# A hybrid decoder layer on one core: norms' root in the output stage, a longer run of products at the switch to the MLP, and more buffers for reloaded activations

## The chip, the cores and the metric

The kernel runs on one core of a Trainium2 chip. The metric is device time in microseconds (us), the median of several executions. A profile of one execution goes with it; its times count from the start of its span.

The engines are TensorE (PE for matmuls, PEld for weight loads), VectorE (DVE), ScalarE (ACT), GpSimd (POOL) and SyncE (SP). SP does no arithmetic here: it is a queue that issues DMA transfers in order. Each engine works through its own list in order, so an instruction that waits holds up everything behind it on that engine.

## The reference, cut to what matters

One decoder layer runs over 1024 prompt tokens and 32 sample tokens (T = 1056 columns, model width 1024, MLP width 4096, all float32). The change lies in the second half of the layer:

```python
x = x + merged @ w_out
h2 = rmsnorm(x, g_ffn)
x = x + jnp.square(jax.nn.relu(h2 @ w_up)) @ w_down
...
y = rmsnorm(x, g_final)
```

## The kernel before, in words

Activations lie transposed, channels on partitions and tokens along the free dimension. The 1056 tokens fall into four column blocks of 264 (CQ), and a "quarter" c (0 or 1) is the pair of blocks (t, c) for t = 0, 1. A float32 product is made of three matmuls: each operand is split into a rounded part (a copy on ACT) and a rest (a subtraction on DVE), and high x high, high x low and low x high are summed in one PSUM bank.

**Output stage** (out_quarter, lines 1167 to 1190). For each quarter, eight row blocks m of x + merged @ w_out are computed. Each adds its squares to `acc` (ACT line 1163, GpSimd line 1164). After each pair of row blocks j, `factors` makes the seven combined right operands of a 2x2x2 fast product (Winograd's form of Strassen) from the pair. The splits in it are line 1133 (ACT) and line 1134 (DVE).

**Up stage** (16 groups, class Up). Group u makes 256 rows of the hidden layer by seven products i = 0 to 6 per quarter. A "unit" is one group for one quarter; a product in it is 12 matmuls of 264 columns (line 1231). Products 0, 3, 5 and 6 sum in one bank `x` and products 2 and 4 in a bank `z`; after each, ACT or DVE copies the bank out, and the next product into that bank waits for the copy. The tokens' norm factors enter in `relu2` (line 1254) as `rb2`. They come from `column_norms`: matmuls with a vector of ones (line 1198), a root and a Newton step (lines 157 to 162), matmuls that spread the result over the partitions (line 1204), a copy into `rb2` (line 1206). The tile of `rb2` takes the memory of `acc`. Hidden values go to DRAM (`ffd`).

**Down stage** (16 windows, class Down). A window accumulates 2 to 4 hidden groups into the 256 output rows `mp`. Its right operands come back from `ffd`: `right` (line 1387) loads one into a buffer "gt" (line 1392, from SP; two buffers), ACT rounds it (line 1394) and DVE makes the rest (line 1395). There are 98 such loads; the last one or two windows' worth are held in 28 of 29 large buffers (slabA with 20, slabB with 9). The residual x returns from DRAM into `accs`, and DVE adds the products to it (lines 1306 to 1309). The weights are factored on ACT and DVE five steps ahead (lines 1341 to 1351). The last 512 hidden rows take an ordinary product at the end, with the final norm.

PSUM has two pools, `mmbank` with three banks and `bank` (tiles "ax") with five. A scheduler in the framework decides each engine's order from priorities in program order and free buffers; it also picks which freed buffer a tile gets.

Of the kernel before, what the change touches and what calls it, by code (L numbers as in the profile page):

```python
# [8 lines left out]
F32 = mybir.dt.float32  # L9
F32R = mybir.dt.float32r  # L10
# [6 lines left out]
P = 128  # L17
# [6 lines left out]
T = SEQ + NS  # L24
# [21 lines left out]
def hybrid_kernel(tc, xt, cache_k, cache_v, h0, norms, w_in, sinks, w_attn_o, lam_re, lam_im, log_dt,  # L46
                  b_ri, b_ir, c_ri, d_cols, w_glu, w_out, w_up, w_down, w_last,
                  y_cols, y_rows, k_prompt, v_prompt, ssm_prompt, k_sample, v_sample, ssm_sample, dbg=None):
    nc = tc.nc
    uid = [0]  # L50

    def new(pool, shape, dt, tag, bufs=None):
        uid[0] += 1
        return pool.tile(list(shape), dt, tag=tag, name=f"{tag}_{uid[0]}", bufs=bufs)
# [3 lines left out]
    wts = es.enter_context(tc.tile_pool(name="wts", bufs=2))  # L58
# [3 lines left out]
    slabA = es.enter_context(tc.tile_pool(name="slabA", bufs=20))  # L62

    def bank(pool=None):
        return new(psax, [P, 512], F32, "ax")

    def mmbank():
        return new(psmm, [P, 512], F32, "mm")
# [11 lines left out]
    ps = bank()  # L80
# [74 lines left out]
    def rsqrt_newton(out, ms, tmp1, tmp2):  # L155

        nc.scalar.activation(tmp1, ms, AF.Sqrt)
        nc.vector.reciprocal(tmp1, tmp1)  # L158
        nc.vector.tensor_tensor(tmp2, tmp1, tmp1, op=ALU.mult)
        nc.vector.tensor_tensor(tmp2, tmp2, ms, op=ALU.mult)  # L160
        nc.vector.tensor_scalar(tmp2, tmp2, -0.5, 1.5, op0=ALU.mult, op1=ALU.add)
        nc.vector.tensor_tensor(out, tmp1, tmp2, op=ALU.mult)
# [360 lines left out]
    with tc.tile_pool(name="ptmp", bufs=1) as pt:  # L523
        with tc.tile_pool(name="start", bufs=1) as st:
            prm = []
            acc = start(st, lambda: prm.extend(s5_small_loads(pt)))
# [3 lines left out]
            ft = s5_params(pt, *prm)  # L530
# [543 lines left out]
    slabB = es.enter_context(tc.tile_pool(name="slabB", bufs=9, side="right", reuse_waits="tile"))  # L1074
# [3 lines left out]
    for k in range(KT):  # L1078
        a = q2[k // 2][:, k % 2]
        h = new(slabB, [P, T], F32R, "slab")  # L1080
        l = new(slabA, [P, T], F32R, "slab")
# [5 lines left out]
    HT, CQ = T // 2, T // 4  # L1087
# [40 lines left out]
    def factors(j, c, x, pools):  # L1128

        V = nc.vector  # L1130

        def split(t, src):
            nc.scalar.copy(t[:, :, 0], src)
            V.tensor_tensor(t[:, :, 1], src, t[:, :, 0].bitcast(F32), op=ALU.subtract)

        b, t14, t3 = (new(p, [P, 2, 2, CQ], F32R, "slab") for p in pools[:3])
        if c == 0:
            odd[j] = new(pools[3], [P, 2, 2, CQ], F32R, "slab")
        split(b, x[:, :, 0])
        V.tensor_tensor(x[:, 0, 0], x[:, 0, 1], x[:, 0, 0], op=ALU.subtract)  # L1140
        t2 = new(wts, [P, 2 * CQ], F32, "gt")[:, :CQ]
        V.tensor_tensor(t2, x[:, 1, 1], x[:, 0, 0], op=ALU.subtract)
        V.tensor_tensor(x[:, 1, 0], x[:, 1, 0], t2, op=ALU.subtract)
        V.tensor_tensor(x[:, 0, 1], x[:, 1, 1], x[:, 0, 1], op=ALU.subtract)
        split(t14, x[:, :, 0])
        split(odd[j][:, c:c + 1], t2.rearrange("p (o f) -> p o f", o=1))
        split(t3, x[:, :, 1])
        h2c[c][j] = [b[:, 0], b[:, 1], t14[:, 0], odd[j][:, c], t3[:, 1], t3[:, 0], t14[:, 1]]
# [23 lines left out]
    def out_quarter(c, last_weights):  # L1172
        w = wblock(w_out, 0)
        for j in range(KT // 2):
            xr = new(gen, [P, 2, 2, CQ], F32, "slab")
            x = new(gen, [P, 2, 2, CQ], F32, "slab")
            for i in range(2):
                m = 2 * j + i
                nc.sync.dma_start(xr[:, i], quarter(xt[m], c))
                last = c == 1 and m == KT - 1  # L1180
                wm = w
                if m + 1 < KT:
                    w = wblock(w_out, m + 1)
                else:
                    last_weights()
                out_tile(wm, m, c, xr[:, i], last or c == m == 0, bank if last else mmbank)
                nc.scalar.activation(x[:, i], xr[:, i], AF.Copy, scale=gcol[:, 1, m:m + 1])
                nc.sync.dma_start(quarter(x2d[j][:, i], c), xr[:, i])
            factors(j, c, x, FPOOLS[c][j])

    def column_norms(c):

        n = CQ // 3
        ms, r, t1, t2 = (small4(6, tag=t, bufs=2) for t in ("nms", "nr", "nt1", "nt2"))
        ps = bank()
        for i in range(6):
            t0 = (i // 3) * HT + c * CQ + (i % 3) * n
            nc.tensor.matmul(ps[:n, i:i + 1], acc[:, t0:t0 + n], ones[:, 0:1], start=True, stop=True)
        nc.vector.tensor_scalar(ms[:n], ps[:n, :6], 1.0 / D, EPS, op0=ALU.mult, op1=ALU.add)
        rsqrt_newton(r[:n], ms[:n], t1[:n], t2[:n])  # L1200
        for t in range(2):
            ps = bank()
            for i in range(3):
                nc.tensor.matmul(ps[:, i * n:i * n + n], r[:n, 3 * t + i:3 * t + i + 1].to_broadcast([n, P]),
                                 ident[:n, :n], start=True, stop=True)
            nc.scalar.copy(rb2[c][:, t], ps[:, :CQ])

# [10 lines left out]
    class Unit:  # L1218
# [15 lines left out]
        def step(self, i):  # L1234
            if i == 0:
                self.x = ps = bank()
            elif i == 1:
                ps = mmbank()
            elif i == 2:
                self.z = ps = mmbank()  # L1240
            else:
                ps = self.z if i == 4 else self.x
            self.prod(ps, i, i < 3)
            self.take(i, ps[:, :CQ])
# [133 lines left out]


    fct = {}  # L1380
    PLACES = [slabA] * 6 + [slabB] * 3 + [slabA] * 2 + [slabB] * 2 + [slabA] * 6 + [slabB] * 2 + [slabA] * 6 + [slabB]
    rights = []
    for n, (_, _, u1) in enumerate(WINDOWS):
        u0 = max([0] + [w[2] for w in WINDOWS[:n]])
# [2 lines left out]
    def right(n):  # L1387

        for _ in range(n):
            u, i = rights.pop(0)  # L1390
            ft = new(wts, [P, 2, CQ], F32, "gt")
            nc.sync.dma_start(ft, ffd[u][:, SLOT[i]])
            f = fct[u, i] = new(PLACES[(7 * u + i) % 28], [P, 2, 2, CQ], F32R, "slab")
            nc.scalar.copy(f[:, 0], ft)  # L1394
            V.tensor_tensor(f[:, 1], ft, f[:, 0].bitcast(F32), op=ALU.subtract)  # L1395
# [4 lines left out]
    rbt = new(const, [P, 2, 2, CQ], F32, "rb")  # L1400
    for c in range(2):
        rb2[c] = rbt[:, c]
    accs = {2: new(accp, [P, 2, T], F32, "acc")}
    nc.sync.dma_start(accs[2], x2d[2])

# [1 line left out]

    def ff_block(f):
        h = new(slabA, [P, T], F32R, "slab")
        l = new(slabB if f < 3 else slabA, [P, T], F32R, "slab")  # L1410
        for t in range(2):
            ts = slice(t * HT, t * HT + HT)
            ft = new(wts, [P, 2, CQ], F32, "gt")
            nc.sync.dma_start(ft, ffd[NSD + f // 2][:, ((0, 3), (1, 2))[f % 2][t]])
            ft = ft.rearrange("p c f -> p (c f)")
            nc.scalar.copy(h[:, ts], ft)
            V.tensor_tensor(l[:, ts], ft, h[:, ts].bitcast(F32), op=ALU.subtract)  # L1417
        ffh.append(h)
        ffl.append(l)

    def last_weights(m):
        raw = new(wts, [P, 2, 4 * P], F32, "raw")[:, 0].rearrange("p (k m) -> p k m", k=FC)
        nc.sync.dma_start(raw, w_last[m])
        wt = new(slabA, [P, 2, FC, P], F32R, "slab")
        nc.scalar.copy(wt[:, 0], raw)
        V.tensor_tensor(wt[:, 1], raw, wt[:, 0].bitcast(F32), op=ALU.subtract)  # L1426
        ws.append((wt[:, 0], wt[:, 1]))

    FC = 4
    rest = [lambda f=f: ff_block(f) for f in range(FC)] + [lambda m=m: last_weights(m) for m in range(KT)]  # L1430
    pend, fresh = [], 0
    for n, g in enumerate(groups):
        d = n - NU_
        if d == 0:
            upp.close()
            accq = es.enter_context(tc.tile_pool(name="accq", bufs=3, reuse_waits="tile"))
            for mp in (3, 0, 1):
                accs[mp] = new(accq, [P, 2, T], F32, "acc")
                nc.sync.dma_start(accs[mp], x2d[mp])
        order = [(i, c) for i in range(6) for c in range(2)]  # L1440
        if n == 0:
            order = [(i, 0) for i in range(4)] + [(i, 1) for i in range(4)] + order[8:]
        before = fresh
        if d >= 0:
            fresh = max(w[2] for w in WINDOWS[:d + 2]) - max(w[2] for w in WINDOWS[:d + 1])
        for i, c in order:
            if n == 0 and i == 0:
                column_norms(c)
            g.units[c].step(i)
            if c == 0:  # L1450
                continue
            left()
            if i == 0 and pend:
                for un in pend:
                    un.step(6)
                left()
                right(before)
            if d == -1:
                right((0, 3, 3, 3, 2, 3)[i])
            right(fresh)  # L1460
            if d >= len(WINDOWS) - 3 and i % 2 and (rest if d > len(WINDOWS) - 3 else len(rest) > KT):
                rest.pop(0)()
        pend = g.units
# [165 lines left out]
```

## Time and profile before

| | |
|---|---|
| median of 3 runs | 1742.67 us (1742.42 to 1746.3) |
| the profiled execution's own time | 1745.46 us |
| its span | 1743.5 us |
| PE busy | 1664.1 us, 95% |
| DVE busy | 1255.8 us, 72% |
| ACT busy | 863.0 us, 49% |
| mean granted TensorE clock | 0.978 of full speed |

Busy time is the time in which at least one instruction of an engine is under way. Matmuls overlap, so the time from one start to the next tells more of PE's pace than the duration of one. The granted clock is 1.00 at 2.4 GHz and 0.50 at 1.2 GHz. An idle time in brackets stands ahead of the instruction that it delayed, with what released it.

### The profile page before, as it was taken

How to read it: one execution, taken by the hardware profiler on the slowest of the kernel's cores; microseconds unless marked ns; L12 is line 12 of the kernel's file. 1: busy time of each engine (PE TensorE's matmuls, PEld its weight loads, DVE VectorE, ACT ScalarE, POOL GpSimd, SP SyncE). 2: the span in 40 equal slices, each digit the busy share in tenths (PEclk: the TensorE clock that was granted, in tenths of full speed). 3: DMA queues.
4: the chain of work that ended last, by engine and by line, in shares of the span. 5: the costliest groups of instructions: out<-in, count | busy, mean ns of one | idle time of the engine just before them, and what ended most of it. 6: DMA issues, size and time to landing. Idle time of an engine off the chain costs nothing. (4 is left out here: it accounts for less than half of the span.)

```text
span 1743.5 us, 30870 instructions
## 1 busy us (share of the span) xinstructions
PE 1664.1 (95%) x11952; PEld 1626.7 (93%) x11952; DVE 1255.8 (72%) x2449; ACT 863.0 (49%) x1878; POOL 287.6 (16%) x250
## 2 busy tenths in 40 slices
PE   6989999999999899999999999999999899999996
PEld 6989999999998888989999999999999899999986
DVE  8898787654488999842644767767776788777767
ACT  5344354332367788753433654444444555454454
POOL 5211111101234344420222320000000000000013
PEclk8999999999999999999999999999999999999998
DMA  5144434433101311133444544444444755453412
GB/s 205 62 149 149 127 94 142 141 110 108 51 25 54 109 50 62 62 123 98 143 132 132 178 144 137 155 148 136 136 148 137 248 159 155 126 165 113 124 55 100
DMA packets 131686, 213.16 MB, mean 122 GB/s; under 512 B 13756, under 2 KB 86540, under 8 KB 131028
## 3 DMA queue, kind: packets, MB, share of 16 engines
q1 hardware_dynamic: 84452, 162.16, 29.4%
q10 hardware_dynamic: 45360, 46.63, 7.9%
q0 software_dynamic: 1728, 2.41, 0.6%
q8 instruction: 93, 1.52, 0.4%
q14 instruction: 53, 0.43, 0.1%
HBM read 146.26 MB, written 64.90 MB: 121 GB/s over the span
## 5 line engine op out<-in xcount | busy, mean ns | idle before, releaser
L118 PE MATMUL mm<-slab,whi 128*128 128x352 f32 (+3 forms) x1688 | 532.0, 315 | 20.6 <-DVE slab L182 12.4
L117 PE MATMUL mm<-slab,whi 128*128 128x352 f32 (+3 forms) x1688 | 537.1, 320 | 8.2 <-DVE Up L435 7.1
L119 PE MATMUL mm<-slab,wlo 128*128 128x352 f32 (+3 forms) x1688 | 531.7, 315 | 0.3 <-DVE wlo L92 0.3
L1231 PE MATMUL ax<-slab,w 128*128 128x264 f32 x2880 | 371.4, 287 | 7.6 <-ACT slab L1394 4.9
L1231 PEld LDWEIGHTS ax<-slab,w 128*128 128x128 f32 x2880 | 360.7, 190 | 10.8 <-ACT slab L1394 5.3
L118 PEld LDWEIGHTS mm<-slab,whi 128*128 128x128 f32 x1688 | 322.4, 191 | 24.3 <-DVE slab L182 13.4
L117 PEld LDWEIGHTS mm<-slab,whi 128*128 128x128 f32 x1688 | 320.8, 190 | 10.9 <-issue 8.2
L119 PEld LDWEIGHTS mm<-slab,wlo 128*128 128x128 f32 x1688 | 321.2, 190 | 0.8 <-DVE wlo L92 0.6
L1231 PE MATMUL mm<-slab,w 128*128 128x264 f32 x2160 | 281.8, 286 | 9.2 <-DVE acc L1306 5.7
L1231 PEld LDWEIGHTS mm<-slab,w 128*128 128x128 f32 x2160 | 271.6, 190 | 11.9 <-DVE acc L1306 7.7
L91 ACT CAST whi<-raw 128x1024 fp32r<-128x1024 f32 x76 | 79.6, 1048 | 101.2 <-PE mm L118 64.9
L1526 POOL TENSOR_TENSOR slab<-slab,slab 128x512 f32<-128x512 f32 x7 | 9.1, 1293 | 659.2 <-ACT slab L1523 659.2
L1342 DVE TENSOR_TENSOR w<-raw,w 128x512 fp32r<-128x512 f32 (+2 forms) x96 | 63.0, 656 | 71.1 <-ACT w L1341 68.9
L92 DVE TENSOR_TENSOR wlo<-raw,whi 128x1024 fp32r<-128x1024 f32 x76 | 99.5, 1309 | 18.9 <-ACT whi L91 18.5
L1394 ACT CAST slab<-gt 128x528 fp32r<-128x528 f32 x98 | 62.0, 634 | 93.1 <-DMA gt<-ffd 91.3
L1395 DVE TENSOR_TENSOR slab<-gt,slab 128x528 fp32r<-128x528 f32 x98 | 68.5, 704 | 38.6 <-ACT slab L1394 38.2
L804 POOL TENSOR_TENSOR qs<-q,qs 64x256 fp32r<-64x256 f32 x64 | 62.9, 983 | 70.6 <-ACT qs L803 59.7
L1341 ACT CAST w<-whi 128x512 fp32r<-128x512 f32 (+2 forms) x64 | 37.9, 593 | 58.6 <-PE ax L1231 28.2
L828 ACT ACTIVATE pm<-pm,sm 128x128 f32<-128x128 f32 x128 | 49.9, 391 | 33.6 <-DVE sm L825 33.4
L1255 ACT ACTIVATE slab<-slab 128x264 f32<-128x264 f32 x80 | 33.9, 425 | 61.8 <-DVE slab L1254 45.4
L843 POOL TENSOR_TENSOR pt<-fb,pt 128x512 fp32r<-128x512 f32 x28 | 41.6, 1485 | 120.2 <-ACT pt L842 76.7
L1341 ACT CAST w<-raw 128x512 fp32r<-128x512 f32 (+2 forms) x96 | 56.9, 593 | 4.8 <-PE mm L1231 2.5
(400 smaller groups left out, 2649.8 us busy)
## 6 DMA issues: line engine op xcount, KB each, us to landing
gt<-ffd SPq DMA_DIRECT2D x106, 264.0 KB
raw<-in_w_in_dram SPq DMA_DIRECT2D x36, 512.0 KB
raw<-in_w_up_dram SPq DMA_DIRECT2D x32, 512.0 KB
ffd<-slab ACTq DMA_DIRECT2D x28, 528.0 KB
raw<-in_w_down_dram SPq DMA_DIRECT2D x22, 512.0 KB
gd<-gt ACTq DMA_DIRECT2D x48, 176.0 KB
slab<-gd SPq DMA_DIRECT2D x16, 528.0 KB
raw<-in_w_glu_dram SPq DMA_DIRECT2D x16, 512.0 KB
```

The lines of the kernel that those rows point to most:

```text
L91: nc.scalar.copy(hi[:, :nk], raw[:, :nk])
L92: nc.vector.tensor_tensor(lo[:, :nk], raw[:, :nk], hi[:, :nk].bitcast(F32), op=ALU.subtract)
L117: nc.tensor.matmul(ps[:, :cw], w[0][:, k, :], ah[k][:, cs], start=(k == 0), stop=False)
L118: nc.tensor.matmul(ps[:, :cw], w[0][:, k, :], al[k][:, cs], start=False, stop=False)
L119: nc.tensor.matmul(ps[:, :cw], w[1][:, k, :], ah[k][:, cs], start=False, stop=(k == nk - 1))
L804: nc.gpsimd.tensor_tensor(qs[b, :, h], q[a, :, bs], qs[a, :, h].bitcast(F32), op=ALU.subtract)
L828: nc.scalar.activation(pm[:, i], pm[:, i], AF.Exp, bias=ng[:, i:i + 1], accum_out=den[:, i:i + 1])
L1231: nc.tensor.matmul(ps[:, :CQ], w[:, wp, js], b[:, bp], start=start and j == k == 0, stop=j == n - 1 and k == 2, skip_group_check=True)
L1341: nc.scalar.copy(t[:, 0], s)
L1342: V.tensor_tensor(t[:, 1], s, t[:, 0].bitcast(F32), op=ALU.subtract)
L1394: nc.scalar.copy(f[:, 0], ft)
L1395: V.tensor_tensor(f[:, 1], ft, f[:, 0].bitcast(F32), op=ALU.subtract)
```

## The change

Five edits. (1) `column_norms` is cut in two: sums and root stay, the spreading becomes `spread_norms`. For quarter 0 the first part is called inside the output stage of quarter 1, after its first pair j = 0. (2) In the first Up group, five products of quarter 0 (before: four) come ahead of the five of quarter 1. (3) Bank z of quarter 1 comes from the five-bank pool. (4) `incoming` hands out loads in turn to the two "gt" buffers and the two halves of a slab, `ring`; the list of large buffers (PLACES) gives up one slab for it, and the two pools' shares at the end of the kernel are shifted to suit. (5) Three of the four residual tiles `accs` are loaded one window ahead each, not all three when the Down stage opens.

```diff
             factors(j, c, x, FPOOLS[c][j])
+            if c == 1 and j == 0:
+                column_norms(0)
+
+    nr = [None, None]
 
     def column_norms(c):
...
         rsqrt_newton(r[:n], ms[:n], t1[:n], t2[:n])
+        nr[c] = r
+
+    def spread_norms(c):
+
+        n = CQ // 3
         for t in range(2):
             ps = bank()
             for i in range(3):
-                nc.tensor.matmul(ps[:, i * n:i * n + n], r[:n, 3 * t + i:3 * t + i + 1].to_broadcast([n, P]),
+                nc.tensor.matmul(ps[:, i * n:i * n + n], nr[c][:n, 3 * t + i:3 * t + i + 1].to_broadcast([n, P]),
                                  ident[:n, :n], start=True, stop=True)
             nc.scalar.copy(rb2[c][:, t], ps[:, :CQ])
...
             elif i == 2:
-                self.z = ps = mmbank()
+                self.z = ps = bank() if self.c else mmbank()
...
-    PLACES = [slabA] * 6 + [slabB] * 3 + [slabA] * 2 + [slabB] * 2 + [slabA] * 6 + [slabB] * 2 + [slabA] * 6 + [slabB]
+    PLACES = [slabA] * 5 + [slabB] * 3 + [slabA] * 2 + [slabB] * 2 + ([slabA] * 6 + [slabB] * 2) * 2
+    turn_ = [0]
+
+    def incoming():
+
+        turn_[0] += 1
+        if turn_[0] % 2:
+            return new(wts, [P, 2, CQ], F32, "gt")
+        return ring[:, turn_[0] // 2 % 2]
...
-            ft = new(wts, [P, 2, CQ], F32, "gt")
+            ft = incoming()
...
+    ring = new(slabA, [P, 2, 2, CQ], F32, "slab")
...
-        l = new(slabB if f < 3 else slabA, [P, T], F32R, "slab")
+        l = new(slabB if f < 2 else slabA, [P, T], F32R, "slab")
...
-        wt = new(slabA, [P, 2, FC, P], F32R, "slab")
+        wt = new(slabB if m in (4, 5) else slabA, [P, 2, FC, P], F32R, "slab")
...
-            for mp in (3, 0, 1):
-                accs[mp] = new(accq, [P, 2, T], F32, "acc")
-                nc.sync.dma_start(accs[mp], x2d[mp])
+        if 0 <= d < 3:
+            mp = WINDOWS[d + 1][0]
+            accs[mp] = new(accq, [P, 2, T], F32, "acc")
+            nc.sync.dma_start(accs[mp], x2d[mp])
...
-            order = [(i, 0) for i in range(4)] + [(i, 1) for i in range(4)] + order[8:]
+            order = [(i, 0) for i in range(5)] + [(i, 1) for i in range(5)] + order[10:]
...
-            if n == 0 and i == 0:
+            if n == 0 and i == 0 and c == 1:
                 column_norms(c)
             g.units[c].step(i)
+            if n == 0 and i == 0:
+                spread_norms(c)
```

The order of instructions is the scheduler's, so three places are shown as it wrote them. First, PE at the switch from the output stage to the Up stage, before. L1198 are the sums for the norms, L1204 the spreading, L1231 the products (one row for each row pair j; the first row of a product is shown). slab_9893 to 9896 are operands of quarter 0, slab_10501 and slab_10978 those of quarter 1 from its first and its last row pair.

```order
L1198 MATMUL ax_11001<-ones_77,rb_9754 88x1 x6
L1231 MATMUL mm_11040<-slab_9893,w_10901 128x264 x3
...
L1231 MATMUL mm_11057<-slab_9894,w_10909 128x264 x3
...
L1231 MATMUL mm_11130<-slab_10501,w_10901 128x264 x3
...
L1231 MATMUL mm_11057<-slab_9895,w_10915 128x264 x3
...
L1231 MATMUL mm_11130<-slab_10978,w_10901 128x264 x2
L1204 MATMUL ax_11015<-ident_72,nr_1622_10998 128x88 x3
L1204 MATMUL ax_11020<-ident_72,nr_1622_10998 128x88 x3
L1231 MATMUL ax_11025<-slab_9893,w_10895 128x264 x3
...
L1198 MATMUL ax_11088<-ones_77,rb_9754 88x1 x6
```

And PE at the same place in the changed kernel, where L1202 are the sums, L1213 the spreading and L1240 the products.

```order
L1240 MATMUL ax_11016<-slab_9893,w_10913 128x264 x3
...
L1213 MATMUL ax_11031<-ident_72,nr_1553_10518 128x88 x3
L1213 MATMUL ax_11036<-ident_72,nr_1553_10518 128x88 x3
L1240 MATMUL mm_11041<-slab_9893,w_10919 128x264 x3
...
L1240 MATMUL mm_11058<-slab_9894,w_10927 128x264 x3
...
L1240 MATMUL ax_11016<-slab_9896,w_10930 128x264 x3
...
L1240 MATMUL mm_11058<-slab_9895,w_10933 128x264 x3
...
L1202 MATMUL ax_11105<-ones_77,rb_9754 88x1 x6
L1240 MATMUL ax_11119<-slab_10501,w_10913 128x264 x3
```

The first operand of quarter 1's last row pair was needed after 45 matmuls of products, and is now needed after 69 and the spreading of quarter 0's norms; quarter 0's sums (L1202) stand inside the output stage.

Second, ACT at the same switch, before: the end of the last output tile (L1163, L1187), the root (L157), the four splits of the last row pair (L1133), the copies of banks and of the norms (L1261, L1206).

```order
L1187 ACTIVATE slab_10822<-slab_10821,gcol_79 128x528
L157 ACT_TABLE_LOAD
L157 ACTIVATE nt_1623_10999<-nms_1621_10997 88x6
L1133 CAST slab_10978<-slab_10822 128x2x264
L1133 CAST slab_10349<-gt_10984 128x264
L1133 CAST slab_10979<-slab_10822 128x2x264
L1133 CAST slab_10980<-slab_10822 128x2x264
L1261 COPY slab_11038<-ax_11025 128x264
L1206 COPY rb_10994<-ax_11015 128x264
```

ACT at that place in the changed kernel; L1278 and L1270 are copies of product banks, L1215 those of the norms.

```order
L1187 ACTIVATE slab_10840<-slab_10839,gcol_79 128x528
L1133 CAST slab_10996<-slab_10840 128x2x264
L1278 COPY slab_11029<-mm_11058 128x264
L1278 COPY slab_11029<-ax_11016 128x264
L1133 CAST slab_10349<-gt_11002 128x264
L1133 CAST slab_10997<-slab_10840 128x2x264
L1133 CAST slab_10998<-slab_10840 128x2x264
L1215 COPY rb_11012<-ax_11031 128x264
```

The table load and the root are gone from ahead of the first split; the copy of bank z (mm_11058) stands behind that split.

Third, SP where the Down stage opens, before. ffd_1433 and ffd_1434 are hidden groups 1 and 2, `acc` the residual tiles, `raw` weight blocks.

```order
L1321 DMA raw_15118<-in_w_down_dram 128x2x384
L1439 DMA acc_15032<-x2d_1431_9737 128x2112
L1392 DMA gt_15023<-ffd_1433_9739 128x528
L1439 DMA acc_15034<-x2d_1428_9734 128x2112
L1439 DMA acc_15036<-x2d_1429_9735 128x2112
L1392 DMA gt_15094<-ffd_1434_9740 128x528
L1392 DMA gt_15120<-ffd_1434_9740 128x528
```

SP there in the changed kernel; slab_11013 is the ring.

```order
L1410 DMA gt_15084<-ffd_1434_9740 128x528
L1410 DMA slab_11013<-ffd_1434_9740 128x528
...
L1410 DMA gt_15184<-ffd_1434_9740 128x528
L1330 DMA raw_15108<-in_w_down_dram 128x2x384
...
L1459 DMA acc_15026<-x2d_1431_9737 128x2112
L1459 DMA acc_15214<-x2d_1428_9734 128x2112
L1330 DMA raw_15161<-in_w_down_dram 128x2x512
L1410 DMA gt_15260<-ffd_1434_9740 128x528
```

Six loads of group 2 now stand ahead of the first residual tile (before: none), and two residual tiles, not three, stand close together.

## Rows read from the trace of the kernel before

**Rows 1.** The page, busy time and instructions of each engine.

```profile
PE 1664.1 (95%) x11952; PEld 1626.7 (93%) x11952; DVE 1255.8 (72%) x2449; ACT 863.0 (49%) x1878; POOL 287.6 (16%) x250
```

**Rows 2.** Who waited for whom, PE alone, whole span (total us, times, longest).

```profile
PE mm L1231 <- DVE acc L1306: 5.7, 7, 1.3
```

**Rows 3.** Stretches: length, busy us (instructions) by engine, clock, DMA share, GB/s.

```profile
1100.00:1200.00 100.00, 100.00 (x822) 100.00 (x821) 72.27 (x151) 44.74 (x104) 0.00 (x0) 1.00 0.44 148
1345.30:1396.60 51.30, 44.41 (x330) 42.73 (x329) 36.90 (x79) 27.25 (x61) 0.00 (x0) 0.93 0.66 219
1396.60:1679.30 282.70, 275.56 (x2222) 271.91 (x2221) 220.59 (x423) 134.85 (x279) 0.00 (x0) 1.00 0.47 136
```

**Rows 4.** Timeline of PE at the switch to Up: start, us, instruction, [idle before].

```profile
1027.60 1.03 PE L1198 MATMUL ax<-ones,rb 128*88 128x1 f32 x12
1028.49 5.71 PE L1231 MATMUL mm<-slab,w 128*128 128x264 f32 x45
1036.45 0.39 PE L1231 MATMUL mm<-slab,w 128*128 128x264 f32 x1 [2.25 <-ACT slab L1133]
1037.36 0.39 PE L1231 MATMUL mm<-slab,w 128*128 128x264 f32 x1 [0.52 <-DVE slab L1134]
1039.52 2.99 PE L1231 MATMUL ax<-slab,w 128*128 128x264 f32 x12
...
1049.44 1.47 PE L1204 MATMUL ax<-ident,nr 88*128 88x88 f32 x12
```

**Rows 5.** PE in steps of 1 us there: busy (instructions), clock, DMA share, GB/s.

```profile
1038.00:1039.00 1.00, 1.00 (x8) 0.56 0.00 0
...
1048.00:1049.00 1.00, 1.00 (x9) 0.82 0.00 0
```

**Rows 6.** Timeline of ACT at the switch to Up.

```profile
1033.64 0.72 ACT L1187 ACTIVATE slab<-slab,gcol 128x528 f32<-128x528 f32 x1
1034.38 1.28 ACT L157 ACT_TABLE_LOAD   x1
...
1035.78 0.61 ACT L1133 CAST slab<-slab 128x528 fp32r<-128x528 f32 x1
```

**Rows 7.** Timeline of DVE: first and last step of quarter 1's root.

```profile
1044.16 0.16 DVE L1199 TENSOR_SCALAR nms<-ax 88x6 f32<-88x6 f32 x1 [0.78 <-PE ax L1198]
...
1048.65 0.16 DVE L162 TENSOR_TENSOR nr<-nt,nt 88x6 f32<-88x6 f32 x1
```

**Rows 8.** Who waited for whom, PE alone, 1360 to 1411 us.

```profile
PE ax L1231 <- ACT slab L1394: 4.9, 2, 3.3
PE ax L1231 <- ACT whi L1303: 1.1, 1, 1.1
...
PE ax L1231 <- DVE slab L1395: 0.5, 1, 0.5
```

**Rows 9.** PE in steps of 1 us at the switch to Down.

```profile
1389.00:1390.00 1.00, 0.00 (x0) 0.85 0.79 234
...
1396.00:1397.00 1.00, 1.00 (x8) 0.74 0.52 76
```

**Rows 10.** Timeline of SP at the switch to Down: start, us, transfers issued.

```profile
1379.03 0.80 SPq L1439 DMA_DIRECT2D acc<-x2d  x2
1380.23 6.70 SPq L1392 DMA_DIRECT2D gt<-ffd  x2
```

**Rows 11.** Timeline of ACT at the switch to Down.

```profile
1378.83 0.63 ACT L1394 CAST slab<-gt 128x528 fp32r<-128x528 f32 x1 [1.73 <-DMA gt<-ffd]
```

**Rows 12.** Who waited for whom, ACT alone, 1400 to 1680 us.

```profile
ACT slab L1394 <- DMA gt<-ffd: 81.5, 57, 3.9
ACT w L1341 <- PE ax L1231: 14.5, 10, 2.3
```

**Rows 13.** Timeline of DVE in a window of the Down stage.

```profile
1498.21 0.71 DVE L1395 TENSOR_TENSOR slab<-gt,slab 128x528 fp32r<-128x528 f32 x1 [1.58 <-ACT slab L1394]
```

**Rows 14.** Timeline of PE at the same place.

```profile
1499.32 0.87 PE L1231 MATMUL mm<-slab,w 128*128 128x264 f32 x5 [1.09 <-DVE acc L1306]
```

More of the change, by code (lines that the diff above doesn't have):

```diff
@@ L1409, in ff_block @@
         h = new(slabA, [P, T], F32R, "slab")
-        l = new(slabB if f < 3 else slabA, [P, T], F32R, "slab")
+        l = new(slabB if f < 2 else slabA, [P, T], F32R, "slab")
         for t in range(2):
             ts = slice(t * HT, t * HT + HT)
-            ft = new(wts, [P, 2, CQ], F32, "gt")
+            ft = incoming()
             nc.sync.dma_start(ft, ffd[NSD + f // 2][:, ((0, 3), (1, 2))[f % 2][t]])
```

## Prediction

> **What bounds the kernel now.** I began with the busy line of the page: PE is busy for 95% of the span and has an instruction under way nearly always [rows 1]. So time can come only from PE's stops and from stretches at half clock. Next, PE's pace where nothing stops it: 822 matmuls in 100 us, 0.1217 us each [rows 3]. From the first product of the Up stage to the end of Down there are 16 x 2 x 7 x 12 = 2688 products' matmuls in Up and 98 x 24 = 2352 in Down, 5040 in all, which would take 613 us. They took from 1028.5 to about 1679.3, 651 us [rows 3, 4]. The norms' small matmuls are about 4 of the difference of 37 us. To find the rest I read the chain of time on PE at the two switches and the waits of PE by stretch. Three places hold 26 us:
>
> *Up switch.* After 45 product matmuls PE waits 2.25 us for a split on ACT and 0.52 us for one on DVE [rows 4]. Then its clock is at 0.50 for nine steps of 1 us, and between the levels in the steps at both ends [rows 5]: 0.56 there means 0.88 us at half, 0.82 means 0.36. So 0.88 + 9 + 0.36 = 10.2 us at half, 5.1 of them lost (12 matmuls take 2.99 us there, against 1.46 at full pace). Lost: 2.8 + 5.1 = 7.9.
>
> *Down switch.* In 1345.3 to 1396.6 PE makes 330 matmuls, 40.2 us of work, in 51.3 us [rows 3]. The waits add to 7.5 us with two small ones, most of them for ACT's rounding of reloaded activations [rows 8]; ACT waits for the transfer [rows 11], and SP took 6.70 us to issue two of them, behind two residual tiles [rows 10]. The clock is at 0.50 for 0.3 + 6 + 0.52 = 6.8 us, read in the same way [rows 9], 3.4 us lost. Together 10.9.
>
> *Down stage.* In 282.7 us PE is busy 275.56, so 7.1 us idle, at a mean clock of 1.00 [rows 3]. 5.7 us are seven waits for DVE's adds from bank z [rows 2]. One of them, followed back: PE waits 1.09 us for the add [rows 14]; just ahead on DVE stands a rest that waited 1.58 us for ACT [rows 13]; ACT waits 57 times for a reload, 81.5 us in all [rows 12]. So these stops too begin with late reloads in two buffers.
>
> **The change part by part.** All sums go against the profile's own time, 1745.46 us (1743.5 of it span). The median is 1742.67; I carry the same gain over to it.
>
> *Edits 1 and 2, Up switch.* Count from the last matmul of the output stage, 1027.6. The new order has 48 product matmuls (5.84 us) and the spreading of quarter 0's norms (1.47 [rows 4]) before the fifth product, which takes bank z: PE is there at 7.3. The copy of z stands on ACT behind the first split. ACT ended L1187 at 1034.36 [rows 6], so at 6.8; split 0.61 [rows 6], copy of half that width, about 0.4: 7.8. A wait of 0.5. Table load and root no longer stand ahead of the split, 1.4 us between L1187's end and the split [rows 6], so the last pair's two operands, which PE got at 8.85 and 9.8 [rows 4], come at 7.4 and 8.4. PE wants the first after 69 matmuls, the spreading and quarter 1's sums (8.4 + 1.47 + 0.9 + the wait of 0.5 = 11.3). They are hidden with 3 us to spare. Late next is quarter 1's own root: the sums end at 10.2, DVE's chain from its first to its last step takes 4.65 us [rows 7], with its start 15.3; PE has 36 matmuls of quarter 1 ahead of the spreading and is there at 14.6. A wait of 0.7, so 1.2 us in place of 2.8, and if the clock stays up 5.1 us at half clock gone: 7.9 - 1.2 = 6.7, I take 6.5. Bounds: 1.6 if the clock falls all the same, 7.9 if neither wait shows. Moved at no cost: quarter 0's sums only change their place on PE (1.03 us either way [rows 4]); the table load of 1.28 us [rows 6] goes to ACT inside the output stage, which PE hides since operands there are made a row pair ahead; if not, it costs at most its 1.28.
>
> *Edits 4 and 5, Down switch.* Six reloads of group 2 are issued before the first residual tile, into four buffers. Residual tile 3 is wanted at once, the next a window later. What ACT waited for [rows 11] is then issued 6 us or more earlier. What remains as a bound is DVE: 36.90 us of work in this stretch [rows 3]. PE without stops would take 40.2 us, and DVE would have to be 92% busy. At 85% the stretch takes 43.4 us, a gain of 7.9; I take 8. Bounds: 3 (the stops shrink, but the clock still falls) and 10.9. The ring costs a large buffer's place, not a holding: 28 tiles are still held. Its first loads wait until the second product of quarter 0 in the last Up group frees the slab, and that is still in the Up stage, where ACT has room (44.74 of 100 us [rows 3]).
>
> *Edits 3 and 4, Down stage.* With four buffers a reload is issued two products earlier; transfers fill 0.47 of the DMA engines' time here [rows 3], so there is room. ACT's 57 waits then mostly hide nothing from PE, and z of quarter 1 has one more chain of products to be freed in. Of 5.7 + 0.6 + 0.6 us of stops I take 5.5 back. Bounds: 1 (the waits move to the next add) and 7.1 (all idle time).
>
> *The end of the kernel*, where the two pools' shares are shifted: the same number of loads of the same sizes, 0; no row speaks of a queue there that the change lengthens.
>
> *Sum:* 6.5 + 8 + 5.5 = 20.0. Profile 1725.5, median 1722.7.
>
> **The rivals.** 0.3%, 5.2 us, is about what a measurement of this kernel can tell from no change.
>
> *The clock falls again at the Up switch.* Two stops of 0.5 and 0.7 us, some 7 us apart, remain. In the rows a stop of 1.09 us left the clock up [rows 14, 3], 2.25 + 0.52 within 1 us lost it [rows 4, 5], and so did 3.3 us with lesser ones [rows 8, 9]. So the rows speak for a clock that stays up, but if my 0.5 is 1.5 they no longer do. Gain 1.6 + 8 + 5.5 = 15.1: 1727.6. Chance 0.17. The Trainium skill (TensorE: Matmul & The Clock Gate, Part 1: The HAM clock gate) says that the monitor of PE's activity runs free of the program, so that where a stop falls in its count is chance; by that the same two stops could cost 5.1 us in one execution and nothing in the next, and this case would be 1727.6 and 1722.7 in turn. No run before shows that, and the rows' durations decide here.
>
> *The Down switch stays late.* DMA carried 219 GB/s at a share of 0.66 in the stretch [rows 3], and 0.79 just ahead of the fall of the clock [rows 9]; moving issues forward changes no byte. If the transfers or DVE are the bound, only 3 come back: 3 + 6.5 + 5.5 = 15.0, 1727.7. Chance 0.11. The share of 0.66 speaks against it. The Trainium skill (DMA: Bandwidth & Descriptors, Issuing engines are not separate DMA queues) has all transfers run on the same 16 engines and interleave, whoever issued them; by that earlier reloads would only take time from the weights in flight, and the time would be this rival's 1727.7. The trace bears that out in part: the share of 0.66 is high, but leaves a third.
>
> *Down's waits move to other adds.* If DVE itself and not the reload is late, a freed z only brings PE to the next bank. DVE is busy 220.59 of 282.7 us, 78% [rows 3], which speaks for it a little; that the followed wait begins at a reload speaks against. 6.5 + 8 + 1 = 15.5: 1727.2. Chance 0.07.
>
> *The change does not do what it says.* The four buffers are handed out in turn, so one late buffer can hold up the three others, and the order of transfers on SP may keep the reloads late; at the Up switch the wait for z may come out at 2 us and more. Then there are new stops in place of the old: gain 0 to 5, 1738 to 1743. Chance 0.07.
>
> *Slower.* With more reloads in hand, ACT takes up their rounding at once, in order, and the weight factors behind them hold PE's next product or wait for PE to free a slab. ACT's waits for slabs freed by PE are 14.5 us in ten, 1.45 each [rows 12]. If each of the 70 reloads after the opening met a third of that, 0.48 us, and PE stood with it, 34 us would be lost and 14.5 of gains at the other places left: 1762. It decides from 0.28 us a reload (70 x 0.28 = 19.6, the 14.4 gained and 5.2 more). Against: weights are factored five steps ahead, ACT is busy 134.85 of 282.7 us [rows 3], and PE has no such wait in its rows. Chance 0.03.
>
> **How the numbers follow.** All three steps: 0.55, 1722.7, with its own range 1715.5 to 1727 (the upper and middle bounds of the terms: 7.9 + 10.9 + 7.1 = 25.9 would be 1716.8, and a little of the 11 us of loss that I gave to no place). The three cases near 1727.5 together 0.35; no effect 0.07; slower 0.03. Faster by over 0.3% is all but the last two, 0.90, of which I give 0.01 to each side's spread: faster 0.89, same 0.07, slower 0.04. The range 1715 to 1733 takes in the two switches missed at once (20.0 - 4.9 - 5 = 10.1, 1732.6), and leaves out the last two cases.
>
> **What would show it.** Up switch: in PE's timeline no stop above 0.8 us between the output stage and the second spreading, granted clock 1.00 in each step of 1 us. Wrong, if steps at 0.50 stand there again or a wait for ACT's copy of z is over 1 us. Down switch: PE's waits for the rounding of reloads fall from 5 to below 2 us in all, and no step at 0.50; the same stretch of 330 matmuls takes about 43 us. Wrong, if a load in the ring is issued late or the first residual tile now stops DVE's adds. Down stage: ACT's waits for reloads fall from 81.5 to below 30 us, and PE's for adds from 5.7 to 1. Wrong, if ACT waits as long as before though it has four buffers, or PE's waits stand at another line with the same sum. The prediction as a whole is wrong if PE's idle time at a place is merely found at another, above all in the last stretch with the ordinary product and the final norm, of which I have counted nothing.

## The result and the profile after

The changed kernel takes 1722.58 us, the median of 4 runs (1719.29 to 1723.68), beside 1743.62 for the kernel before (4 runs). The ratio is 0.9866, interval 0.9845 to 0.9887: faster by 1.3%. The profiled execution takes 1723.68 us, its span is 1720.6.

Line numbers have moved: the products are L1240 now (L1231 before), the sums L1202, the spreading L1213, ACT's rounding of a reload L1412 and DVE's rest of it L1413, DVE's add L1315. The busy line of the page, to be laid beside [rows 1]:

```profile
PE 1652.6 (96%) x11952; PEld 1618.7 (94%) x11952; DVE 1254.6 (73%) x2449; ACT 865.1 (50%) x1878; POOL 288.6 (17%) x250
```

The same instructions, and PE is busy for 11.5 us less. PE's timeline at the Up switch (start, us, instruction, idle before), against [rows 4]:

```profile
1030.20 1.63 PE L1240 MATMUL ax<-slab,w 128*128 128x264 f32 x12
1031.67 1.47 PE L1213 MATMUL ax<-ident,nr 88*128 88x88 f32 x12
1032.92 3.16 PE L1240 MATMUL mm<-slab,w 128*128 128x264 f32 x24
...
1037.94 1.73 PE L1240 MATMUL mm<-slab,w 128*128 128x264 f32 x12 [0.39 <-ACT slab L1278]
1039.51 1.03 PE L1202 MATMUL ax<-ones,rb 128*88 128x1 f32 x12
...
1045.45 1.54 PE L1213 MATMUL ax<-ident,nr 88*128 88x88 f32 x12 [0.30 <-DVE nr L162]
```

Two short stops are left: the fifth product waits for the copy of bank z, and the second spreading for quarter 1's root. Neither costs the clock, as PE in steps of 1 us shows at both (busy, clock, DMA share, GB/s), against [rows 5]:

```profile
1037.00:1038.00 1.00, 0.61 (x6) 1.00 0.52 176
1038.00:1039.00 1.00, 1.00 (x8) 1.00 0.00 0
1045.00:1046.00 1.00, 0.70 (x7) 1.00 0.00 0
```

ACT there has no table load ahead of the split, and z's copy right behind it, against [rows 6]:

```profile
1036.22 0.72 ACT L1187 ACTIVATE slab<-slab,gcol 128x528 f32<-128x528 f32 x1
1036.98 0.63 ACT L1133 CAST slab<-slab 128x528 fp32r<-128x528 f32 x1
1037.52 0.37 ACT L1278 COPY slab<-mm 128x264 f32<-128x264 f32 x1
```

The Down switch and the Down stage, cut at the same product matmuls as in [rows 3] (length, then busy us of PE, PEld, DVE, ACT and POOL, clock, DMA share, GB/s):

```profile
1340.10:1383.90 43.80, 40.95 (x330) 40.19 (x329) 35.35 (x77) 27.55 (x64) 0.00 (x0) 1.00 0.80 261
1383.90:1656.70 272.80, 271.55 (x2219) 270.52 (x2218) 219.46 (x426) 136.96 (x275) 0.00 (x0) 1.00 0.46 140
```

PE's waits in the two stretches (total us, times, longest): the switch, against [rows 8], and then the stage, against [rows 2].

```profile
PE ax L1240 <- DVE acc L1315: 1.4, 1, 1.4
PE mm L1240 <- DVE w L1351: 1.2, 1, 1.2
PE mm L1240 <- ACT whi L1312: 0.3, 1, 0.3
```

```profile
PE ax L1240 <- DVE acc L1315: 1.2, 2, 1.0
```

ACT's waits in the stage, for reloads in the small buffers and in the ring, where [rows 12] had 81.5 us in 57:

```profile
ACT slab L1412 <- DMA gt<-ffd: 9.0, 7, 1.8
...
ACT slab L1412 <- DMA slab<-ffd: 1.6, 2, 1.4
```

By the starts of the same matmuls in both traces: from the first to the 169th product matmul (the Up switch) 25.58 us in place of 32.41, from the 2500th to the 2828th (the Down switch) 43.81 in place of 51.38, from there to the last 272.83 in place of 282.27. That is 6.8 + 7.6 + 9.4 = 23.8. The spans differ by 22.9. The changed kernel's first product starts 1.7 us later, and 1.6 of that stands already at 990 us, ahead of all that the change touches; 0.1 comes back between the two switches and 0.7 behind the last product, so what was saved is not lost again in the end. (Quarter 0's sums stand ahead of the first product in both kernels.) The executions' times differ by 21.8, because the time outside the span is 3.1 us here and was 2.0.

### The profile page after: what moved, and what is told of

It reads as the page before. It is cut to its first block, busy times and chain, and to the rows that moved or that the text cites. A ratio compares the mean times of both kernels' runs of the same rounds, so it can differ in the third digit from the quotient of the medians.

```text
span 1720.6 us, 30881 instructions
## 1 busy us (share of the span) xinstructions
PE 1652.6 (96%) x11952; PEld 1618.7 (94%) x11952; DVE 1254.6 (73%) x2449; ACT 865.1 (50%) x1878; POOL 288.6 (17%) x250
## 5 line engine op out<-in xcount | busy, mean ns | idle before, releaser
L117 PE MATMUL mm<-slab,whi 128*128 128x352 f32 (+3 forms) x1688 | 537.2, 320 | 10.2 <-DVE Up L435 8.1
L1240 PE MATMUL ax<-slab,w 128*128 128x264 f32 x3600 | 452.0, 285 | 2.6 <-DVE acc L1315 2.5
L1240 PEld LDWEIGHTS ax<-slab,w 128*128 128x128 f32 x3600 | 443.9, 188 | 4.0 <-DVE acc L1315 3.7
L1240 PE MATMUL mm<-slab,w 128*128 128x264 f32 x1440 | 186.7, 284 | 1.9 <-DVE w L1351 1.2
L1240 PEld LDWEIGHTS mm<-slab,w 128*128 128x128 f32 x1440 | 179.8, 188 | 2.5 <-DVE w L1351 1.4
L1351 DVE TENSOR_TENSOR w<-raw,w 128x512 fp32r<-128x512 f32 (+2 forms) x96 | 63.0, 657 | 77.2 <-ACT w L1350 75.4
L568 POOL TENSOR_TENSOR tmp<-bbs,TP 128x1024 f32<-128x1024 f32 x8 | 20.6, 2576 | 206.5 <-DVE W L557 206.5
L1351 DVE TENSOR_TENSOR w<-wlo,w 128x512 fp32r<-128x512 f32 (+2 forms) x64 | 42.1, 658 | 5.4 <-ACT w L1350 4.4
```

The costliest lines, as they stand in the source:

```text
L117: nc.tensor.matmul(ps[:, :cw], w[0][:, k, :], ah[k][:, cs], start=(k == 0), stop=False)
L1240: nc.tensor.matmul(ps[:, :CQ], w[:, wp, js], b[:, bp], start=start and j == k == 0, stop=j == n - 1 and k == 2, skip_group_check=True)
L1351: V.tensor_tensor(t[:, 1], s, t[:, 0].bitcast(F32), op=ALU.subtract)
```

## The experiments

Each kernel was run in five rounds beside the kernel before on the same chip. The three columns of stretches come from one profiled execution of each and are cut as above; "less" is one minus the ratio, times the median of before beside it (1743.62 for the first result, then 1745.03, 1746.83 and 1745.35 for the groups of four that follow).

| kernel | ratio (interval) | less, us | Up switch | Down switch | Down stage |
|---|---|---|---|---|---|
| before | | | 32.41 | 51.38 | 282.27 |
| changed, first result | 0.9866 (0.9845, 0.9887) | 23.4 | 25.58 | 43.81 | 272.83 |
| edits 1 and 2 (e1_norms_five) | 0.9959 (0.9944, 0.9975) | 7.2 | 25.42 | 53.03 | 280.91 |
| edit 3 (e2_z) | 0.9996 (0.9984, 1.0009) | 0.7 | 30.99 | 50.60 | 282.19 |
| edit 4 (e3_ring) | 0.9896 (0.9877, 0.9915) | 18.1 | 29.52 | 44.33 | 271.90 |
| edit 5 (e4_acc) | 0.9983 (0.9965, 1.0001) | 3.0 | 29.69 | 48.35 | 283.85 |
| changed again (k_full) | 0.9872 (0.9843, 0.9901) | 22.4 | 25.57 | 43.60 | 272.12 |
| edits 1 and 4 (k_ring_root) | 0.9874 (0.9846, 0.9902) | 22.0 | 25.21 | 43.68 | 273.75 |
| changed without 4 (u_ring) | 0.9949 (0.9931, 0.9968) | 8.9 | 25.61 | 48.18 | 283.23 |
| edit 1 (v_root) | 0.9970 (0.9951, 0.9989) | 5.2 | 25.22 | 53.12 | 281.20 |
| edit 2 (v_five) | 0.9998 (0.9982, 1.0014) | 0.3 | 27.96 | 51.66 | 281.90 |
| edit 1, three buffers (d3_three) | 0.9924 (0.9910, 0.9939) | 13.3 | 25.21 | 51.78 | 274.59 |
| tiles two products later (g_late2) | 0.9872 (0.9856, 0.9888) | 22.3 | 25.57 | 44.26 | 271.94 |
| some rests on GpSimd (g_pool) | 0.9869 (0.9851, 0.9886) | 22.9 | 25.57 | 43.97 | 272.42 |

**Each edit alone.** The kernel before with the lines of edits 1 and 2:

```diff
+            if c == 1 and j == 0:
+                column_norms(0)
...
-            order = [(i, 0) for i in range(4)] + [(i, 1) for i in range(4)] + order[8:]
+            order = [(i, 0) for i in range(5)] + [(i, 1) for i in range(5)] + order[10:]
```

> The kernel before with edits 1 and 2 alone (root of quarter 0's norms in the output stage, five products ahead). My theory: the two stops at the Up switch and the half clock behind them go, and nothing else: 6.8 us less than before, 1736.8 (1734.5 to 1739), granted clock 1.00 in each step of 1 us from 1028 to 1056. Rival, the clock is kept up in the changed kernel by something else than these two edits (it falls again here): 1.6 us less, 1742.

It gains 7.2 us, and the Up switch is 7.0 us shorter, at clock 1.00. The theory stands. The Down switch is 1.7 us longer here than in the trace of before, with as much half clock, and again with the root alone (v_root, below); that was not followed up. Then z's bank:

```diff
-                self.z = ps = mmbank()
+                self.z = ps = bank() if self.c else mmbank()
```

> The kernel before with edit 3 alone (bank z of quarter 1 from the five-bank pool, still two buffers for reloads). My theory: late reloads are the cause of Down's stops, so z alone removes some 2 us of them (1741.6) and ACT's waits for reloads stay near 80 us. Rival, the bank is the cause: PE's waits for the adds in Down go as in the changed kernel, 9.4 us less, 1734, with ACT's waits for reloads as before.

Nothing that can be told from no change, and the Down stage is as long as before. ACT waits for reloads as before, over 1401 to 1683.5 us:

```profile
ACT slab L1394 <- DMA gt<-ffd: 83.2, 57, 3.6
```

The bank is not the cause; my 2 us for it were too many. Then the ring alone:

```diff
-            ft = new(wts, [P, 2, CQ], F32, "gt")
+            ft = incoming()
...
+    ring = new(slabA, [P, 2, 2, CQ], F32, "slab")
```

> The kernel before with edit 4 alone (four buffers for reloads, z in its old bank, three residual tiles at once). My theory: ACT's waits for reloads in Down fall below 20 us and most of Down's 9.4 us come back, and half of the 7.6 us at the Down switch: 13 us less, 1730.6 (1728 to 1734). Rival, the bank is the cause: at most 4 us less, 1739.6, with PE's waits for adds of some 5 us still there.

18.1 us, more than I expected: 1727.03 us is below the range. ACT's waits for reloads, over 1383 to 1655 us, and the stretches, as above:

```profile
ACT slab L1403 <- DMA gt<-ffd: 11.9, 9, 1.6
...
ACT slab L1403 <- DMA slab<-ffd: 1.2, 4, 0.6
```

```profile
1338.60:1382.90 44.30, 40.99 (x331) 40.17 (x329) 35.32 (x77) 27.50 (x64) 0.00 (x0) 1.00 0.81 271
1382.90:1654.80 271.90, 271.60 (x2219) 270.73 (x2218) 219.78 (x425) 137.66 (x275) 0.00 (x0) 1.00 0.46 138
```

All of the Down stage's gain and all but half a microsecond of the Down switch's come with the ring alone: 7.1 + 10.4 = 17.4 in this trace. The expectation gave the ring only half of the switch, and that was wrong; the three residual tiles still stand in a row on SP here. Last the residual tiles:

```diff
-            for mp in (3, 0, 1):
+        if 0 <= d < 3:
+            mp = WINDOWS[d + 1][0]
```

> The kernel before with edit 5 alone (residual tiles spread over the windows, two buffers for reloads). My theory: with two buffers only two reloads can stand ahead of the tiles, so 2 to 3 us come back at the Down switch, 1741 (1739 to 1743). Rival, the three tiles in a row on SP are the whole cause there: 7.6 us less, 1736, and no step at half clock near 1390.

The Down switch is 3.0 us shorter in this trace, as expected, but most of that is clock, which the expectation did not count. The fall comes so late that the stretch holds 1.5 us at half clock where before had 6.8:

```profile
1390.79:1392.26 1.47, 1.26 (x5) 1.26 (x6) 1.26 (x3) 0.10 (x1) 0.00 (x0) 0.50 0.97 383
```

That is up to 2.7 us less lost. The Down stage behind it is 1.6 us longer than before, and the time as a whole is unclear (the interval reaches 1.0001). So a gain by this edit is not shown.

**Together and without.** Three kernels of known edits and the changed kernel once more, on one chip. First edits 1 and 4 only, whose lines are above:

> The changed kernel once more, beside the next three. Theory after the first four runs: the ring of four buffers and the root in the output stage carry all of it; 1745 less 18 and 7 would be 1720, and the changed kernel measured 1722.6. Rival, the spread residual tiles and z's bank add 3 us to what the ring gives.

> The kernel before with edit 4 and the root in the output stage alone (no fifth product, z in its old bank, three residual tiles at once). Theory: within 2 us of the changed kernel, 1721. Rival: 3 us or more above it, with PE's waits for adds from z back in Down.

Two of the five edits give 22.0 us where all five give 22.4. The rival, 3 us from edits 3 and 5, does not show. Without the ring (edits 1, 2, 3 and 5 on two buffers):

> The changed kernel without edit 4 (two buffers for reloads). Theory: only the Up switch is better and a little at the Down switch, 7 + 3 us below the kernel before, 1735 (1732 to 1738), ACT's waits for reloads in Down near 80 us. Rival, z's bank and the spread tiles give most of Down: 1726.

8.9 us, as the theory had it, and the Down stage is as long as before, with PE busy longer again (1.7 us of that by 3.4 us at half clock, from 1391.98 us on):

```profile
1391.10:1674.40 283.30, 277.18 (x2219) 272.98 (x2219) 223.16 (x428) 135.51 (x282) 0.00 (x0) 0.99 0.48 138
```

Then the root without the fifth product:

> The kernel before with the root of quarter 0 in the output stage, still four products ahead. Theory: PE comes to the last pair's operand after 57 matmuls, the spreading and the sums, at 9.3 us after the output stage's last matmul, and the operand is there at 7.4: no stop, clock 1.00, the same 7.5 us as edits 1 and 2 together (1737.5). Rival, the fifth product is needed: a stop of over 1 us stays, and with it some us at half clock, 1741.

The Up switch is 25.22 us, no longer than with both, with one stop of 0.8 us for the norms. By the ratios 5.2 and 7.2 can't be told apart. So the root is the edit that counts there.

**The rest.** The fifth product without the root:

> The kernel before with edit 2 alone (five products ahead, the root still ahead of the last splits on ACT). Theory: it adds no cover by itself, since the first operand of the last row pair is still wanted after 45 matmuls: the stop of some 2 us and steps at 0.50 stay, 1746 like before. Rival, the longer run of products is what keeps the clock: 1740, no step at 0.50 between the output stage and the second spreading.

The time is as before, and the two stops stay. But in the profiled execution the clock did not fall, as the rival had it. PE's timeline, and PE in steps of 1 us:

```profile
1035.47 0.39 PE L1231 MATMUL mm<-slab,w 128*128 128x264 f32 x1 [1.78 <-ACT slab L1133]
1036.38 0.39 PE L1231 MATMUL mm<-slab,w 128*128 128x264 f32 x1 [0.52 <-DVE slab L1134]
```

```profile
1035.00:1036.00 1.00, 0.39 (x1) 1.00 0.00 0
1036.00:1037.00 1.00, 0.62 (x5) 1.00 0.00 0
1037.00:1038.00 1.00, 1.00 (x11) 1.00 0.00 0
```

One trace can't tell the rival from chance: the first stop is a little shorter here, 1.78 us where four other traces have 2.25 to 2.38, and the clock differs among those four too (see below). The mean granted clock of all executions says more. It is 0.9793 here (12 executions), 0.9786 in before (17 beside them), but 0.9807 with the root alone and 0.9814 with edits 1 and 2 (12 each), where the mean itself is known to about 0.0006. So the root keeps the clock up, and that five products alone do is not shown. Three buffers instead of four:

```diff
+        if turn_[0] % 3:
+            return new(wts, [P, 2, CQ], F32, "gt")
+        return ring[:, 0]
```

> The kernel before with the root in the output stage and three buffers for reloads (two gt and one half of the ring) in place of four, nothing else of the change. Theory: what counts is that a reload is issued a product earlier, and the third buffer gives half or more of it: 1731 (1726 to 1736), ACT's waits for reloads in Down between 20 and 60 us. Rival, three already hide the transfer: 1721.5 like four.

1731.04 us, on the theory's number, but not split evenly over the two places. Beside v_root, the same with two buffers, the third gives 6.6 us in the Down stage and 1.3 at the Down switch; beside k_ring_root, which differs in the fourth buffer and in nothing else, the fourth gives 0.8 and 8.1. At the Down switch PE now waits for a weight's rounding and an add:

```profile
1342.30:1394.00 51.70, 43.40 (x330) 42.20 (x329) 37.74 (x82) 28.25 (x65) 0.00 (x0) 0.94 0.71 233
1394.00:1668.60 274.60, 272.69 (x2219) 271.25 (x2218) 217.64 (x421) 134.98 (x274) 0.00 (x0) 1.00 0.46 136
```

```profile
PE mm L1240 <- ACT w L1350: 4.0, 1, 4.0
PE mm L1240 <- DVE acc L1315: 2.4, 1, 2.4
```

Why three buffers leave the switch as late as two was not settled. The last two runs look for what bounds the changed kernel at the Down switch, where DVE waits for weights:

```profile
1374.31 0.56 DVE L1355 TENSOR_TENSOR whi<-raw 128x384 f32<-128x384 f32 x1 [3.08 <-DMA raw<-in_w_down_dram]
```

One moves the residual tiles:

```diff
-        if 0 <= d < 3:
+            if 0 <= d < 3 and i == 2:
```

> The changed kernel with each of the three residual tiles asked for two products later in its window. Theory: at the Down switch DVE now stands 2.95 us for weights whose transfer shares the DMA engines with two residual tiles issued right behind it; with one tile there the stop behind it (1.3 + 1.0 us on PE) shrinks and the 328 matmuls of the stretch take 42 us in place of 43.6; the whole 1720, within what can be told from 1721.8. Rival, DVE's work is the bound there: 43.6 as before, the stop at another line.

One tile, not two, is issued behind the weights, and DVE's wait is the same:

```profile
1374.24 0.56 DVE L1355 TENSOR_TENSOR whi<-raw 128x384 f32<-128x384 f32 x1 [3.09 <-DMA raw<-in_w_down_dram]
```

The theory falls: the second tile's bytes do not hold the weights. The other moves rests to GpSimd:

```diff
-            V.tensor_tensor(f[:, 1], ft, f[:, 0].bitcast(F32), op=ALU.subtract)
+            e = nc.gpsimd if 18 <= 7 * u + i < 36 and i % 3 == 0 else V
+            e.tensor_tensor(f[:, 1], ft, f[:, 0].bitcast(F32), op=ALU.subtract)
```

> The changed kernel with the rests of six of the reloads around the Down switch made on GpSimd, which is idle there, in place of DVE. Theory (the weights' transfer is what DVE waits for): no less than 43.3 us for the stretch. Rival, DVE's work is the bound: 4 us of DVE less, the stretch 42 us or less.

The stretch is 43.97 us, but this tells nothing of DVE there: the lines move eight rests, not six, and all of them came behind it, the first on GpSimd at 1385.23 us, after the stretch's end at 1383.65. In the changed kernel SP issued the late weights at 1369.23 us, when DVE's last reader of that buffer (L1351, 1368.79) was through. That this buffer is the next limit was read from the trace, and not tried. Neither of the two runs beats the changed kernel by what can be measured.

## Why the prediction was right, and where its terms were off

The forecast was 1722.7 us and 1722.58 was measured, but the terms did not come out as evenly as the sum.

*Up switch: 6.5 forecast, 6.8 in the two traces.* Both stops came where the text put them, 0.39 for 0.5 and 0.30 for 0.7 us, with the causes named. Two points of the step don't hold. The credit is the root's alone: v_root, with four products ahead, is as short. And the 5.1 us of half clock were a property of the one trace. Four traces have the old order at this place, with a first stop of 2.25 to 2.38 us and a second of 0.32 to 0.52, and their half-clock time is 10.2 us (before), 6.8 (e2_z), 3.4 (e3_ring) and 3.4 (e4_acc), so that the switch lasts 32.4 to 29.5 us; v_five, with a first stop of 1.78, has none and lasts 28.0. Against the mean of the four, 30.7, the gain is 5.0 to 5.4; the times of whole kernels, 5.2 (v_root) and 7.2 (edits 1 and 2), don't tell that from 6.5. That 6.8 came so close to 6.5 is in part the luck of the trace. The Trainium skill (TensorE: Matmul & The Clock Gate, Part 1: The HAM clock gate) says that the activity monitor runs free of the program. The four traces agree: like stops cost from 1.7 to 5.1 us. The text had used this rule only for a rival that loses the gain in the changed kernel; it says as much of what there was to win. In the changed kernel's traces and those of the others with the root moved (nine in all) the Up switch lasts 25.2 to 25.6 us.

*Down switch: 8 forecast, 7.6 in the two traces.* The ring did it, 7.1 us alone. The clock does not fall there in any of the six traces with four buffers, and falls in all eight with two or three (in u_ring just behind the stretch). The step counted edits 4 and 5 together, but edit 5 gives nothing that shows beside the ring (43.68 without it, 43.60 and 43.81 with it), and alone its gain is not shown. One row was misread: the 6.70 us of [rows 10] are not spent on issuing. The two issues take 0.32 us each, and SP waits between them, at first for a reload to land (2.6 us) and then for DVE. In shorter windows of SP and DVE:

```profile
1380.23 0.32 SPq L1392 DMA_DIRECT2D gt<-ffd  x1
1386.61 0.32 SPq L1392 DMA_DIRECT2D gt<-ffd  x1
```

```profile
1385.89 0.70 DVE L1395 TENSOR_TENSOR slab<-gt,slab 128x528 fp32r<-128x528 f32 x1
```

The second issue follows right behind the end of that subtraction, DVE's last reading of an earlier reload: it was late for want of a free buffer. The 8 itself came from an assumed 85% for DVE. DVE was busy for 35.35 of 43.80 us, 81%, and stood 3 us of it for a weight's transfer, which the text did not name, so the size was met partly by luck. The bound that was feared, transfers, was already there: the mean share of 0.66 hides 13 us with a share of 1.02, in which PE made only 69 matmuls, 8.4 us of work.

```profile
1376.00:1389.00 13.00, 9.38 (x69) 8.32 (x67) 10.35 (x22) 4.71 (x10) 0.00 (x0) 1.00 1.02 392
```

The changed kernel moves about the same bytes (261 GB/s for 43.8 us, 219 for 51.3 before: 11.4 and 11.2 MB), but starts them earlier: the share rose from 0.66 to 0.80, and the stretch still became shorter, so that the rival of the late switch did not come.

*Down stage: 5.5 forecast, bounds 1 to 7.1, 9.4 measured.* This is the mis-sized term, and its upper bound was wrong. The step took PE's idle time, 7.1 us, for all that could be lost. But PE's busy time fell too, as the same matmuls show, cut from the 2828th product matmul to the last, before and then after:

```profile
1396.71:1678.98 282.27, 275.13 (x2219) 271.48 (x2218) 220.26 (x422) 134.60 (x278) 0.00 (x0) 1.00 0.47 136
1383.91:1656.74 272.83, 271.58 (x2219) 270.55 (x2218) 219.49 (x425) 136.96 (x275) 0.00 (x0) 1.00 0.46 140
```

Idle time fell by 5.9 us, near the forecast, and busy time by 3.5. A stop does not only leave a gap. At the stop of [rows 14], PE's timeline in shorter windows:

```profile
1497.83 0.40 PE L1231 MATMUL mm<-slab,w 128*128 128x264 f32 x2
1499.32 0.39 PE L1231 MATMUL mm<-slab,w 128*128 128x264 f32 x1 [1.09 <-DVE acc L1306]
1499.54 0.41 PE L1231 MATMUL mm<-slab,w 128*128 128x264 f32 x2
```

The profile counts 1.09 us idle, but the start of the stopped matmul lies 1.37 us behind the start of the one before it (the second of the two, 0.12 behind 1497.83), where 0.12 is the pace, and the next follows after 0.22: 1.25 + 0.10 us lost, 0.26 more than the idle time. The stage had thirteen stops and now has three, nearly all with 0.26 to 0.28 us of this kind. The ten that are gone make 2.7 of the 3.5 us; the rest was not traced. The cause was right, late reloads: ACT's waits for them fell from 81.5 to 10.6 us (below 30 was forecast) and PE's for adds to 1.2 (about 1). That z's bank helps was wrong: alone it changes nothing.

*The rivals' rows.* The 14.5 us of [rows 12] are not waits for slabs: `w` is a rounded weight. ACT's waits for slabs that PE frees, 0.6 us in [rows 12]'s window, did grow to 18.8 in 18, much as the rival of a slower kernel had it, but PE did not stand with them. And the "11 us of loss that I gave to no place" counts the 4 us of the norms' matmuls, which are work; 7 are left.

So the terms sum to 23.8, not 20.0. The changed kernel's two comparisons give 23.4 and 22.4 by the ratio, 21.0 by the first medians. So the gain was larger than forecast by 1.0 to 3.4 us, and the forecast met the median closely by luck: it started from 1742.67, the median of three runs of the kernel before, which measured 1743.62 with a fourth run and 1745.03 to 1746.83 in the later groups.

## What to carry to other kernels

Where an engine waits late for many small transfers, ask first how many buffers stand between issue and use: here four in place of two took out the waits at two places (three did most of it at one of them, and little at the other), for which the changed kernel also moved a bank and spread other loads without further gain. Do the edits one at a time before crediting a sum of them. And measure what a stop on TensorE costs from start to start at a steady pace, in more than one trace, since idle time leaves out part of it and one trace's half-clock time may be chance.

## What was not expected of the hardware

The same two stops at the Up switch, 2.25 and 0.52 us in before, 2.26 and 0.52 in e3_ring, left PE at half clock for 10.2 us in one execution and for 3.4 in the other. Of the thirteen stops in the Down stage, twelve cost 0.26 to 0.28 us beyond their idle time. And the part ahead of the switch, the same in before, e2_z, e3_ring, e4_acc and v_five, ends anywhere between 1024.7 us (e3_ring's first product) and 1034.6 (e2_z's): 10 us of spread that no edit here touches, about twice the gain of the Up switch, which is why that gain needs the traces besides the times.
